# Gate and up weights of a mixture of experts in rows of 16 KB and transfers of 2 MB

## The chip, the cores and the metric

The kernel runs on one core of a Trainium2 chip. The core has a matrix engine (PE, TensorE), a vector engine (DVE), a scalar engine (ACT), GpSimd (POOL) and a sync engine (SP) that issues transfers; 16 DMA engines move data between HBM and the on-chip memory SBUF. The metric is the time of one execution on the device in microseconds (us), the median of several runs.

## The reference, cut to what matters

A trunk of two layers on 256 tokens of width 1024, all in float32. Each layer mixes the tokens in three parallel branches (one wide input projection, three token mixers, an output projection), adds a LayerNorm, and then runs a mixture of 32 experts, of which a token uses two:

```python
def _hier_moe(x, w_rg, b_rg, w_re, b_re, w_gate, w_up, w_down):
...
    for e in range(N_EXPERTS):
        h = jax.nn.silu(xt @ w_gate[e]) * (xt @ w_up[e])
        y = y + combine[:, e:e + 1] * (h @ w_down[e])
    return y.reshape(bsz, s, d)
```

`w_gate` and `w_up` are 1024 x 512 for each expert, `w_down` is 512 x 1024: 2 MB each, so 6 MB for an expert and 192 MB for a layer's experts. All of them are read in each execution.

## The kernel before

A layer has two stages. In the **mixer stage** PE multiplies the activations with the input projection and the branch projections, whose weights come in transfers of 512 KB (rows of 4 KB for each of 128 partitions): 76 of `w_in` and 24 of `w_br` in a layer. In the **expert stage** the 32 experts go in eight sets i = 0 to 7 of four experts (`EQ`). A set moves 8 MB of gate weights, 8 MB of up weights and 8 MB of down weights.

For a set, `set_front` builds a one-hot matrix `oh` that picks up to 32 tokens for each of the four experts, and its `gather` multiplies it with `x` (tile `pxg`, copied into `xg`), so that each expert's tokens stand in 32 columns. `set_mlp` multiplies `xg` with the gate weights (tile `pg`) and with the up weights (tile `pu`); the loop over the eight pieces k of the 1024 channels is outside, the loop over the four experts inside. `hr` is silu(gate) times up. `set_tail` transposes it (`pht`, `ht`) and multiplies it with the down weights in two halves (`pdn`, `os`), and `set_scatter` adds the result onto the tokens (`acc`). Set 4 begins behind a branch (`overflow`), for the case that an expert has more tokens than places; it isn't taken with these inputs. The last set's down weights come in smaller pieces (1/2 MB and 1/4 MB). After the last set come LayerNorm and the next layer's mixers.

A transfer of gate or up weights (`W`) takes 1 MB: `rows(src, u)` reads two pieces of an expert's weights as 128 rows of 8 KB. So a partition holds other channels than a plain tile would; `ROW(k)` gives the matching permutation of the channels of `x` for the gather, in pieces of 64 columns.

All weights go through a ring of places in SBUF (`ring`, list `places`): 24 places of 8 KB a partition, 9 of them always there (`wp`), and 6, 2 and 7 (`wb`, `wd`, `wc`) that are opened when the mixers' buffers are closed (`more_places`, at the positions `AT`) and closed again by `fewer_places` after the last set. A new transfer waits until the last reader of its place is done. SP issues all transfers in one order; a transfer that waits holds up those behind it. A transfer also waits for an earlier one through its completion counter, of which there are eight in turn (`DMAHW0` to `DMAHW7` in the order rows), so up to eight are in flight.

The order in which each engine's instructions stand is not written by hand: a scheduler of the framework sets it from the program when it is built. Two other loads matter below: `mixer_constants` reads `mc`, 128 rows of 9,500 bytes (1187.5 KB) that the next layer's mixers use, into the memory that the closed pools leave; `W_ln` reads the LayerNorm's parameters into a place of the ring.

Of the kernel before, what the change touches and what calls it, by code (L numbers as in the profile page):

```python
# [10 lines left out]
F32 = mybir.dt.float32  # L11
# [11 lines left out]
KD = D // 128  # L23
EPS = 1e-6
ALPHA = (2 * L) ** 0.25
NE = 32
WP, WB, WC = 9, 6, 7
SP, MX, MS, MB, WD = 8, 20, 6, 4, 2
AT = 4, 6, 7
AHEAD = 2  # L30
HP = 15
BUSY = 3
# [4 lines left out]
EQ = 4  # L37
# [79 lines left out]
def bc(ap, n):  # L117

    return ap.to_broadcast(list(ap.shape[:-1]) + [n])
# [42 lines left out]
def trunk_kernel(ctx: ExitStack, tc: tile.TileContext, x_in, w_in, w_br, w_g, w_u, w_d, smalls, lnp, consts, out,  # L162
                 dbg=None, layers=L, thresh=PL):
    nc = tc.nc
# [6 lines left out]
    wp = ctx.enter_context(tc.tile_pool(name="wp", bufs=WP))  # L171
# [3 lines left out]
    cnt = [0]  # L175
    pools = {}

    def open_pool(name, bufs, side):
        cnt[0] += 1
        cm = tc.tile_pool(name=f"{name}{cnt[0]}", bufs=bufs, side=side, reuse_waits="tile")  # L180
        pools[name] = (cm, cm.__enter__())

    def close_pool(name):
        pools.pop(name)[0].__exit__(None, None, None)
# [15 lines left out]


    places = ["wp"] * WP

    def ring(name="w"):
        cnt[0] += 1
        k = places.pop(0)
        places.append(k)
        return (wp if k == "wp" else pools[k][1]).tile([128, 2048], F32, name=f"{name}{cnt[0]}", tag="w")

    def more_places(name, n, side, at):  # L210
        open_pool(name, n, side)
        places[at:at] = [name] * n
# [2 lines left out]
        close_pool(name)  # L215
        places[:] = [k for k in places if k != name]

    def rows(src, u):

        return src[u:u + 2].rearrange("u p f -> (u p f)").rearrange("(q f) -> q f", f=2048)  # L220

    def ROW(k):

        u, j, kk = k // 4, k // 2 % 2, k % 2
        return lambda a: [a.rearrange("p (u h k q j) -> p u h k q j", h=2, k=2, q=64, j=2)[:, u, h, kk, :, j] for h in range(2)]

    def W(src):
        w = ring()
        nc.sync.dma_start(w, src)
        return w  # L230

# [28 lines left out]
    def mm(o, l, r, start=True, stop=True):  # L260
        return PE.matmul(o, l, r, start=start, stop=stop)  # L261

    def act(o, i, f=AF.Copy, **k):
        return ACT.activation(o, i, f, **k)  # L264
# [6 lines left out]
    def tap(name, ap):  # L271
        if dbg is not None and name in dbg:
            nc.sync.dma_start(dbg[name], ap)
# [7 lines left out]
    x = cp.tile([128, NT, D], F32, name="x")  # L281
# [121 lines left out]
    for l in range(layers):  # L403
# [676 lines left out]
        src = {n: w_in[l, i] for i, (n, _) in enumerate(BLOCKS)}  # L1080
# [94 lines left out]
        def after(n):  # L1175
# [27 lines left out]
            if n == "mC1":  # L1203
                close_pool("mb")
                open_pool("hq", 4, "right")
                more_places("wd", WD, "left", AT[1])
            if n == "o0":
                gb.append(W_ln(l, 0))
            if n == "mA":
                wv.drain("C")  # L1210
                close_pool("mc")
                close_pool("mx")
                more_places("wb", WB, "left", AT[0])

# [21 lines left out]
        close_pool("sb")  # L1236
        more_places("wc", WC, "left", AT[2])
        tap("x1", x)
# [74 lines left out]


        def set_front(i):
            e = EQ * i
            oh = T("oh")
            ohv = oh.rearrange("p (u t e s) -> p u t e s", u=2, t=2, e=EQ)
            it = C["iota"][:, None, None, 0:PL].to_broadcast([128, 2, EQ, PL])
            DVE.tensor_tensor(ohv[:, 0], it, bc(pv[:, :, e:e + EQ, None], PL), op=OP.is_equal)  # L1320
            POOL.tensor_mul(ohv[:, 1], ohv[:, 0], bc(cv[:, :, e:e + EQ, None], PL))  # L1321

            def gather(k0, n, copy, pin=False):

                p, t = P("pxg"), T("xg")
                for k in range(n):
                    for tt in range(NT):
                        for hh, xc in enumerate(ROW(k0 + k)(x[:, tt])):
                            m = mm(p[64 * hh:64 * hh + 64, k * 128:(k + 1) * 128], xc,
                                   oh[:, tt * 128:(tt + 1) * 128], tt == 0, tt == 1)  # L1330
                            if pin and k + tt + hh == 0:
                                tc.keep_in_program_order(m)
                copy(t[:, :n * 128], p[:, :n * 128])
                return [t[:, k * 128:(k + 1) * 128] for k in range(n)]

            def back():
                pt = P("pct")
                for tt in range(NT):
                    PE.transpose(pt[:, tt * 128:(tt + 1) * 128], oh[:, 256 + tt * 128:256 + (tt + 1) * 128], ident)
                ct = T("pct")  # L1340
                act(ct[:, :256], pt[:, :256])
                return ct

            return gather, back

        def set_mlp(i, xg, more=None):
            e = EQ * i
            pg, pu = P("pg"), P("pu")
            for p, src in ((pg, w_g), (pu, w_u)):
                for k in range(KD):  # L1350
                    if k == len(xg):
                        xg += more(k)
                    if k % 4 == 0:
                        ws = [W(rows(src[l, e + a], k // 2)).rearrange("p (k f) -> p k f", k=4) for a in range(EQ)]
                    for a in range(EQ):
                        ps = slice(PL * a, PL * a + PL)
                        mm(p[ps], xg[k][:, ps], ws[a][:, k % 4], k == 0, k == KD - 1)
            h = T("h")
            s = act(h, pg, AF.Silu)
            if i == NB - 1:  # L1360
                ln_exp_after(s)

            hr = T("hr")
            for hh in range(2):
                v = lambda a: a.rearrange("p (h k q j) -> p h k q j", h=2, k=2, q=64)[:, hh]
                DVE.tensor_mul(hr.rearrange("p (j k h q) -> p h k q j", j=2, k=2, h=2)[:, hh], v(h), v(pu))  # L1366
            return hr
# [41 lines left out]
        def overflow(mxi):  # L1409
            cov = M(64, "lg")  # L1410
            DVE.tensor_scalar(cov, posm, thresh + 0.5, None, op0=OP.is_gt)
            DVE.tensor_mul(cov, cov, cmb)
            covv = cov.rearrange("p (t e) -> p t e", t=2)
            rv = nc.values_load(mxi[0:1, 0:1], min_val=0, max_val=S)
            with tc.If(rv > thresh):
                with tc.For_i(0, NE, 1) as ei:

                    room = [wp.tile([128, 2048], F32, name=f"wo{cnt[0]}_{j}", tag="w") for j in range(WP)]
                    ws = []
                    for src in (w_g, w_u, w_d):  # L1420
                        ws.append([])
                        for u in range(4):
                            if u % 2 == 0:
                                both = room.pop()
                            w = both[:, u % 2 * 1024:u % 2 * 1024 + 1024]
                            POOL.dma_start(w, src[l, bass.ds(ei, 1), u].rearrange("e p f -> p (e f)"))
                            ws[-1].append(w)
                    for tt in range(NT):
                        own = [o[:, c:c + 512] for o in (room.pop(),) for c in (0, 512, 1024, 1536)]
                        xt = x_T(tt, own[:2])  # L1430
                        pg, pu = P("og"), P("ou")
                        for p, w in ((pg, ws[0]), (pu, ws[1])):
                            for k in range(KD):
                                mm(p, xt(k), w[k // 2][:, k % 2 * 512:k % 2 * 512 + 512], k == 0, k == 7)
                        h = own[2]
                        act(h, pg, AF.Silu)
                        DVE.tensor_mul(h, h, pu)
                        pt = P("opt")
                        for f in range(4):
                            PE.transpose(pt[:, f * 128:(f + 1) * 128], h[:, f * 128:(f + 1) * 128], ident)  # L1440
                        ht = own[3]
                        DVE.tensor_copy(ht, pt)
                        for hf in range(2):
                            po = P("opd")
                            for f in range(4):
                                mm(po, ht[:, f * 128:(f + 1) * 128],
                                   ws[2][2 * hf + f // 2][:, f % 2 * 512:f % 2 * 512 + 512], f == 0, f == 3)
                            DVE.tensor_scalar_mul(own[hf], po, covv[:, tt, bass.ds(ei, 1)])
                            mm(pacc[tt, hf], ident, own[hf], False, False)

        gather, back = set_front(0)
        xg = gather(0, 2, DVE.tensor_copy) + gather(2, 2, act)
# [12 lines left out]
        for i in range(NB):  # L1465
# [4 lines left out]
            if i == 0:  # L1470

                h = set_mlp(i, xg, lambda k: gather(k, k, act, True))
                ct = back()
                mxi = largest()
            else:
                ct, xg = nxt
                h = set_mlp(i, xg)
            if i + 1 < NB:
                gather, back = set_front(i + 1)
                xg = gather(0, 4, DVE.tensor_copy) + gather(4, 4, act)  # L1480
# [83 lines left out]
```

## Time and profile before

| | |
|---|---|
| median of 3 runs | 1631.17 us (1630.39 to 1631.46) |
| the profiled execution's own time | 1631.13 us |
| its span, first to last instruction | 1629.5 us |
| busy share of PE / DVE / ACT / POOL | 84% / 39% / 31% / 12% |
| mean rate of the DMA engines | 318 GB/s over the span |
| layer 0: mixers, experts | about 18 to 365 us, 385 to 812 us |
| layer 1: mixers, experts | about 823 to 1173 us, 1193 to 1630 us |

The profiled execution stands 0.04 us from the median, so sums made against its time hold for the median too. The span leaves out 1.6 us around the first and last instruction. The stages' limits are the times between which PE or the DMA engines work without a break; between them lie the LayerNorms, the router and the first one-hot matrices.

### The profile page before, as it was taken

What the parts mean: (1) busy time and instruction counts of PE and PEld (TensorE: products, weight loads), DVE (VectorE), ACT (ScalarE), POOL (GpSimd) and SP (SyncE); (2) the same over time, 40 slices, a digit from 0 to 9 for tenths busy, and PEclk for the clock granted to TensorE, in tenths of its full rate; (3) what the DMA queues carried; (4) which work ended last, traced back from release to release, by engine and by line L of the source; (5) the groups of instructions that cost most, each with busy time, mean ns of one, the idle gap of its engine ahead of it and who ended that gap; (6) DMA issues with size and microseconds to landing.
All of it is one profiled execution on the core that took longest, in us unless ns stands there. A gap on an engine that the chain in (4) does not pass through costs nothing.

```text
span 1629.5 us, 25989 instructions
## 1 busy us (share of the span) xinstructions
PE 1371.3 (84%) x10670; PEld 877.0 (54%) x10670; DVE 634.8 (39%) x1194; ACT 504.1 (31%) x997; POOL 188.2 (12%) x158
## 2 busy tenths in 40 slices
PE   8999999999877728866799999999998677287775
PEld 8999878985312203211289998799843122132211
DVE  6887777763000000000188887776620000000002
ACT  5846657541000000000067565685310000000000
POOL 0230243200000000000014212422000000000000
PEclk9999999999989959989899999999999999699889
DMA  9543333879999999999984443348799999999996
GB/s 382 182 155 130 129 131 105 317 292 411 427 427 426 427 426 426 426 427 426 409 318 132 144 141 104 134 141 346 293 408 427 428 425 426 427 427 426 427 427 257
DMA packets 90411, 518.96 MB, mean 318 GB/s; under 512 B 10032, under 2 KB 10672, under 8 KB 42928
## 3 DMA queue, kind: packets, MB, share of 16 engines
q1 hardware_dynamic: 90288, 517.25, 78.9%
q8 instruction: 86, 1.41, 0.3%
q14 instruction: 37, 0.30, 0.1%
HBM read 516.16 MB, written 1.05 MB: 317 GB/s over the span
## 4 chain that ended last, share of the span: by engine, by line
DMA 49%; PE 46%; DVE 3%; issue 1%; ACT 1%; SPq 0%; DVEq 0%
DMA w<-in_w_u_dram 19%; DMA w<-in_w_g_dram 14%; DMA w<-in_w_d_dram 14%; PE g L261 9%; PE pbr L261 6%; PE cx L261 3%; PE cz L261 3%; PE pout L261 3%; PE aq L261 1%; PE cbc L261 1%; PE av L261 1%; PE bq L261 1%; PE ak L261 1%; PE az L261 1%; PE bg L261 1%; PE pdn L261 1%
## 5 line engine op out<-in xcount | busy, mean ns | idle before, releaser
L252 DVE TENSOR_TENSOR hi<-w,hi 128x512 fp32r<-128x512 f32 x400 | 324.5, 828 | 84.2 <-ACT hi L264 37.4
L1366 DVE TENSOR_TENSOR hr<-h,pu 128x256 f32<-128x256 f32 x32 | 16.7, 599 | 726.7 <-PE pu L261 726.7
L264 ACT ACTIVATE hi<-w 128x512 fp32r<-128x512 f32 x400 | 242.8, 629 | 144.1 <-PE pbr L261 35.8
L261 PE MATMUL pg<-w,xg 128*32 128x512 f32 x1024 | 190.4, 667 | 114.4 <-DMA w<-in_w_g_dram 114.2
L261 PE MATMUL pu<-w,xg 128*32 128x512 f32 x1024 | 194.1, 673 | 61.1 <-DMA w<-in_w_u_dram 61.1
L261 PEld LDWEIGHTS pg<-w,xg 128*32 128x32 f32 x1024 | 43.7, 119 | 245.7 <-issue 138.2
L261 PE MATMUL pdn<-w,ht 128*32 128x512 f32 x1024 | 145.6, 614 | 26.5 <-DMA w<-in_w_d_dram 13.7
L261 PEld LDWEIGHTS pu<-w,xg 128*32 128x32 f32 x1024 | 45.6, 120 | 190.1 <-DMA w<-in_w_u_dram 110.0
L261 PE MATMUL g<-xh,hi 128*128 128x256 f32 x768 | 143.4, 285 | 0.0
L261 PEld LDWEIGHTS g<-xh,hi 128*128 128x128 f32 x768 | 120.7, 191 | 6.2 <-issue 5.8
L264 ACT ACTIVATE h<-pg 128x512 f32<-128x512 f32 x16 | 9.6, 597 | 338.7 <-PE pg L261 338.7
L261 PE MATMUL g<-xl,hi 128*128 128x256 f32 x384 | 108.9, 284 | 0.0
L261 PEld LDWEIGHTS pdn<-w,ht 128*32 128x32 f32 x1024 | 36.4, 112 | 121.8 <-issue 71.7
L1321 POOL TENSOR_TENSOR oh<-oh,cmb 128x256 f32<-128x256 f32 x16 | 10.0, 623 | 760.2 <-DVE oh L1320 654.9
L261 PE MATMUL pbr<-yh,hi 128*128 128x256 f32 x512 | 95.4, 283 | 0.0
L264 ACT ACTIVATE xg<-pxg 128x512 f32<-128x512 f32 (+1 forms) x18 | 10.3, 574 | 247.5 <-PE pxg L261 247.5
L264 ACT ACTIVATE os<-pdn 128x512 f32<-128x512 f32 x32 | 19.1, 596 | 215.7 <-PE pdn L261 140.9
L261 PEld LDWEIGHTS pbr<-yh,hi 128*128 128x128 f32 x512 | 80.4, 190 | 0.8 <-issue 0.3
L261 PE MATMUL pxg<-oh,x 128*64 128x128 f32 x1024 | 59.9, 274 | 21.9 <-DVE oh L1320 18.3
L261 PEld LDWEIGHTS pxg<-oh,x 128*64 128x64 f32 x1024 | 56.0, 138 | 34.9 <-issue 26.2
L261 PEld LDWEIGHTS g<-xl,hi 128*128 128x128 f32 x384 | 73.5, 191 | 0.1
L261 PE MATMUL pbr<-yl,hi 128*128 128x256 f32 x256 | 73.0, 285 | 0.0
(351 smaller groups left out, 2209.2 us busy)
## 6 DMA issues: line engine op xcount, KB each, us to landing
w<-in_w_g_dram SPq DMA_DIRECT2D x128, 1024.0 KB, 19.5
w<-in_w_u_dram SPq DMA_DIRECT2D x128, 1024.0 KB, 19.6
w<-in_w_d_dram SPq DMA_DIRECT2D x112, 1024.0 KB, 19.6
w<-in_w_in_dram SPq DMA_DIRECT2D x152, 512.0 KB, 4.7
w<-in_w_br_dram SPq DMA_DIRECT2D x48, 512.0 KB, 4.7
w<-in_w_d_dram SPq DMA_DIRECT2D x24, 512.0 KB, 11.8
ln<-in_lnp_dram SPq DMA_DIRECT2D x8, 512.0 KB, 10.7
w<-in_w_d_dram SPq DMA_DIRECT2D x16, 256.0 KB, 7.5
```

The lines of the kernel that those rows point to most:

```text
L252: return DVE.tensor_sub(l, src, lo(h))
L261: return PE.matmul(o, l, r, start=start, stop=stop)
L264: return ACT.activation(o, i, f, **k)
L1321: POOL.tensor_mul(ohv[:, 1], ohv[:, 0], bc(cv[:, :, e:e + EQ, None], PL))
L1366: DVE.tensor_mul(hr.rearrange("p (j k h q) -> p h k q j", j=2, k=2, h=2)[:, hh], v(h), v(pu))
```

## The change

Twelve places of 16 KB take the place of 24 places of 8 KB; the memory is the same. `unit` hands out a whole place, `ring` half of one, two in a row from the same place. Sets 1 to 7 load gate and up weights with `W2`: one transfer of 2 MB for an expert's whole matrix, 128 rows of 16 KB. Set 0 keeps its transfers of 1 MB. The gather of sets 1 to 7 works in pieces of 32 columns instead of 64, twice as many. Down weights, mixer weights and LayerNorm parameters keep their transfers, in halves of a place; a place is free again only when both halves are read.

```diff
-WP, WB, WC = 9, 6, 7
-SP, MX, MS, MB, WD = 8, 20, 6, 4, 2
-AT = 4, 6, 7
+WP, WB, WC = 4, 3, 4
+SP, MX, MS, MB, WD = 8, 24, 6, 4, 1
+AT = 2, 3, 4
...
-    def ring(name="w"):
+    halves = []
+
+    def unit(name="w"):
+
+        assert not halves
         cnt[0] += 1
         k = places.pop(0)
         places.append(k)
-        return (wp if k == "wp" else pools[k][1]).tile([128, 2048], F32, name=f"{name}{cnt[0]}", tag="w")
+        return (wp if k == "wp" else pools[k][1]).tile([128, 4096], F32, name=f"{name}{cnt[0]}", tag="w")
+
+    def ring(name="w"):
+
+        if not halves:
+            w = unit(name)
+            halves.extend((w[:, 0:2048], w[:, 2048:4096]))
+        return halves.pop(0)
...
-    def rows(src, u):
-
-        return src[u:u + 2].rearrange("u p f -> (u p f)").rearrange("(q f) -> q f", f=2048)
-
-    def ROW(k):
-
-        u, j, kk = k // 4, k // 2 % 2, k % 2
-        return lambda a: [a.rearrange("p (u h k q j) -> p u h k q j", h=2, k=2, q=64, j=2)[:, u, h, kk, :, j] for h in range(2)]
+    def rows(src, u, n=2):
+
+        return src[u:u + n].rearrange("u p f -> (u p f)").rearrange("(q f) -> q f", f=1024 * n)
+
+    def ROW(k, n):
+
+        u, j, kk = k // (2 * n), k // 2 % n, k % 2
+        return lambda a: [a.rearrange("p (u h k q j) -> p u h k q j", h=n, k=2, q=128 // n, j=n)[:, u, h, kk, :, j]
+                          for h in range(n)]
...
+    def W2(src):
+        w = unit()
+        nc.sync.dma_start(w, src)
+        return w
...
-            e = EQ * i
+            e, nr = EQ * i, 2 if i == 0 else 4
...
-                    if k % 4 == 0:
+
+                    if i == 0 and k % 4 == 0:
                         ws = [W(rows(src[l, e + a], k // 2)).rearrange("p (k f) -> p k f", k=4) for a in range(EQ)]
+                    elif k == 0:
+                        ws = [W2(rows(src[l, e + a], 0, 4)).rearrange("p (k f) -> p k f", k=8) for a in range(EQ)]
                     for a in range(EQ):
                         ps = slice(PL * a, PL * a + PL)
-                        mm(p[ps], xg[k][:, ps], ws[a][:, k % 4], k == 0, k == KD - 1)
+                        mm(p[ps], xg[k][:, ps], ws[a][:, k % (4 if i == 0 else 8)], k == 0, k == KD - 1)
```

The diff leaves out three lines of the gather that use `nr` and one that cuts the places of the branch into halves. The order of the instructions changes at some places; three follow. In the rows `w_…` are places of the ring, `in_w_g_dram`, `in_w_u_dram` and `in_w_d_dram` the gate, up and down weights in HBM; the shape is that of the transfer or of the operand.

**SP at the end of layer 0.** The last down weights of set 7, then the next layer's loads (`sb` and `mc` are the mixers' small parameters and constants). Before:

```order
L1377 DMA w_6579<-in_w_d_dram 128x512
L538 DMA w_6711<-in_w_in_dram 128x1024 x2
L538 DMA w_6782<-in_w_in_dram 128x1024 x2
L538 DMA w_6889<-in_w_in_dram 128x1024 x2
L294 DMA sb_6628<-in_smalls_dram 128x393
L538 DMA w_6997<-in_w_in_dram 128x1024 x2
L538 DMA w_7076<-in_w_in_dram 128x1024 x2
L538 DMA w_7155<-in_w_in_dram 128x1024 x2
L538 DMA w_7234<-in_w_in_dram 128x1024 x2
L538 DMA w_7335<-in_w_in_dram 128x1024 x2
L538 DMA w_7462<-in_w_in_dram 128x1024 x2
L300 DMA mc_6887<-in_consts_dram 128x2375
```

Of the change, the same place:

```order
L1396 DMA w_6618<-in_w_d_dram 128x1024 x2
L1396 DMA w_6618<-in_w_d_dram 128x512 x4
L316 DMA mc_6926<-in_consts_dram 128x2375
L1396 DMA w_6619<-in_w_d_dram 128x1024 x2
L1396 DMA w_6619<-in_w_d_dram 128x512 x4
L554 DMA w_6751<-in_w_in_dram 128x1024 x4
L310 DMA sb_6668<-in_smalls_dram 128x393
```

`mc` stood behind the last down weights and 18 transfers of `w_in`; it now stands ahead of the last 2 MB of down weights.

**PE and SP in layer 0's set 7.** SP's transfers of the change for set 7, gate (`g`) and up (`u`) weights and the LayerNorm's parameters (`ln`):

```order
L245 DMA w_6497<-in_w_g_dram 128x4096
L245 DMA w_6531<-in_w_u_dram 128x4096
L245 DMA w_6533<-in_w_u_dram 128x4096
L245 DMA w_6535<-in_w_u_dram 128x4096
L253 DMA ln_6486<-in_lnp_dram 128x1024 x2
L245 DMA w_6491<-in_w_g_dram 128x4096
L245 DMA w_6493<-in_w_g_dram 128x4096
L245 DMA w_6495<-in_w_g_dram 128x4096
L245 DMA w_6537<-in_w_u_dram 128x4096
L1396 DMA w_6589<-in_w_d_dram 128x1024 x4
```

PE's first matmuls of that set, in the change:

```order
L277 MATMUL pg_6489<-w_6491,xg_6351 32x512
L277 MATMUL pu_6490<-w_6531,xg_6351 32x512
L277 MATMUL pu_6490<-w_6533,xg_6351 32x512
L277 MATMUL pu_6490<-w_6535,xg_6351 32x512
L277 MATMUL pg_6489<-w_6493,xg_6351 32x512
L277 MATMUL pg_6489<-w_6495,xg_6351 32x512
L277 MATMUL pg_6489<-w_6497,xg_6351 32x512
L277 MATMUL pg_6489<-w_6491,xg_6351 32x512
```

Before, SP loaded the set's eight transfers of gate, then eight of up weights, and PE could do half of `pg` with the first four. Now PE's sixth matmul needs the gate place `w_6495`, the seventh of the set's eight gate and up transfers, and 29 matmuls of `pg` and 29 of `pu` stand behind it.

**SP and PE in set 4, around the branch.** Behind the branch SP of the change issues:

```order
L245 DMA w_5810<-in_w_g_dram 128x4096
L245 DMA w_5814<-in_w_g_dram 128x4096
L245 DMA w_5816<-in_w_g_dram 128x4096
L240 DMA w_6013<-in_w_d_dram 128x2048 x2
L245 DMA w_6076<-in_w_u_dram 128x4096
```

Set 4's other gate place `w_5812`, its four up places and six of its eight transfers of down weights stand ahead of the branch. PE's first matmuls of the set, in the change:

```order
L277 MATMUL pg_5808<-w_5810,xg_5523 32x512
L277 MATMUL pg_5808<-w_5812,xg_5523 32x512
L277 MATMUL pu_5809<-w_5850,xg_5523 32x512
L277 MATMUL pu_5809<-w_5852,xg_5523 32x512
```

Set 4 was split by the branch before, too: three gate, seven up and five down transfers of 1 MB ahead of it, the other five gate, one up and three down behind it. In the change PE's first matmul of the set needs a place that is loaded behind the branch, and the whole of the set's work stands behind that matmul; `w_6076` is set 5's first.

## Rows read from the trace of the kernel before

**Rows 1.** The page: span, busy shares, tracks of PE and DMA, the chain's shares.

```profile
span 1629.5 us, 25989 instructions
PE 1371.3 (84%) x10670; PEld 877.0 (54%) x10670; DVE 634.8 (39%) x1194; ACT 504.1 (31%) x997; POOL 188.2 (12%) x158
...
PE   8999999999877728866799999999998677287775
...
DMA  9543333879999999999984443348799999999996
...
DMA 49%; PE 46%; DVE 3%; issue 1%; ACT 1%; SPq 0%; DVEq 0%
```

**Rows 2.** Windows of the four stages: busy us, PE's clock, DMA share, GB/s.

```profile
18.00:365.00 347.00, 345.35 (x2986) 314.39 (x2986) 268.08 (x478) 216.58 (x432) 85.14 (x66) 1.00 0.54 195
385.00:812.00 427.00, 311.44 (x2104) 104.41 (x2105) 23.59 (x46) 24.49 (x43) 4.32 (x7) 0.90 1.01 424
823.00:1173.00 350.00, 349.39 (x3033) 318.33 (x3022) 271.82 (x485) 218.47 (x435) 86.33 (x67) 1.00 0.51 185
1193.00:1630.00 437.00, 307.39 (x2100) 101.70 (x2096) 29.96 (x58) 25.16 (x45) 7.40 (x9) 0.91 0.97 409
```

**Rows 3.** The chain that ended last, in layer 0's experts: start, us, what.

```profile
428.13 19.54 DMA w<-in_w_d_dram
...
447.73 19.56 DMA w<-in_w_g_dram
...
467.35 19.56 DMA w<-in_w_u_dram
```

**Rows 4.** What SP waited for, 400 to 760 us: us, times, longest.

```profile
SPq L229 <- DMA w<-in_w_u_dram: 99.2, 48, 2.5
SPq L229 <- DMA w<-in_w_g_dram: 96.4, 47, 3.2
SPq L229 <- DMA w<-in_w_d_dram: 95.0, 46, 2.2
SPq L229 <- PE pu L261: 6.2, 5, 4.8
```

**Rows 5.** Windows with rows of 4 KB (the first) and of 8 KB (the others).

```profile
826.00:832.00 6.00, 6.00 (x53) 6.00 (x52) 4.80 (x14) 3.92 (x11) 0.00 (x0) 1.00 1.02 422
440.00:560.00 120.00, 90.52 (x552) 27.32 (x547) 5.35 (x10) 5.33 (x10) 1.23 (x2) 0.90 1.01 426
611.20:616.00 4.80, 4.80 (x50) 2.20 (x47) 0.00 (x0) 0.00 (x0) 0.00 (x0) 1.00 1.03 434
606.00:611.20 5.20, 5.11 (x25) 1.73 (x28) 0.00 (x0) 0.00 (x0) 0.00 (x0) 0.50 1.00 424
580.50:611.20 30.70, 5.11 (x25) 1.73 (x28) 0.00 (x0) 0.00 (x0) 0.00 (x0) 0.50 1.01 427
```

**Rows 6.** The chain at the end of layer 1: last set and LayerNorm.

```profile
1551.22 2.56 PE pdn L261 x21
1553.78 20.26 DMA w<-in_w_g_dram
...
1574.10 19.51 DMA w<-in_w_u_dram
...
1593.62 9.97 DMA w<-in_w_d_dram
...
1603.66 8.18 DMA w<-in_w_d_dram
...
1611.88 3.68 PE pdn L261 x28
```

**Rows 7.** DMA packets, 829.9 to 830.6 us, while `mc` lands among `w_in`.

```profile
DMA packets 51, 0.29 MB, mean 408 GB/s; under 512 B 5, under 2 KB 5, under 8 KB 33
```

**Rows 8.** Tile `mc`: forms, counts, ns min/median/max, first and last start.

```profile
L300 SPq DMA_DIRECT2D mc<-in_consts_dram x2: 327/484/642, 6.2 to 821.0; - x2
L261 PE MATMUL cum<-ev,mc x16: 197/282/283, 45.5 to 853.6; 128*128 128x40 f32 x16
```

**Rows 9.** Timeline of PE in layer 1's last set: idle time before in brackets.

```profile
1593.65 3.62 PE L261 MATMUL pu<-w,xg 128*32 128x512 f32 x26 [1.46 <-DMA w<-in_w_u_dram]
...
1599.97 3.41 PE L261 MATMUL pdn<-w,ht 128*32 128x512 f32 x22 [0.78 <-DVE ht L1385]
...
1611.88 3.63 PE L261 MATMUL pdn<-w,ht 128*32 128x512 f32 x28 [2.24 <-DMA w<-in_w_d_dram]
```

**Rows 10.** Timeline of PE behind the branch of set 4, layer 0.

```profile
606.09 1.07 PE L261 MATMUL pg<-w,xg 128*32 128x512 f32 x3 [28.32 <-DMA w<-in_w_g_dram]
```

**Rows 11.** DMA issues on the page: KB each, median us from issue to landing.

```profile
w<-in_w_in_dram SPq DMA_DIRECT2D x152, 512.0 KB, 4.7
```

**Rows 12.** Groups of the page: the gather's matmuls.

```profile
L261 PE MATMUL pxg<-oh,x 128*64 128x128 f32 x1024 | 59.9, 274 | 21.9 <-DVE oh L1320 18.3
```

More of the change, by code (lines that the diff above doesn't have):

```diff
@@ L1327, in gather @@
                     for tt in range(NT):
-                        for hh, xc in enumerate(ROW(k0 + k)(x[:, tt])):
-                            m = mm(p[64 * hh:64 * hh + 64, k * 128:(k + 1) * 128], xc,
+                        for hh, xc in enumerate(ROW(k0 + k, nr)(x[:, tt])):
+                            m = mm(p[128 // nr * hh:128 // nr * (hh + 1), k * 128:(k + 1) * 128], xc,
                                    oh[:, tt * 128:(tt + 1) * 128], tt == 0, tt == 1)
@@ L1416, in overflow @@
                 with tc.For_i(0, NE, 1) as ei:
-                    room = [wp.tile([128, 2048], F32, name=f"wo{cnt[0]}_{j}", tag="w") for j in range(WP)]
+                    room = [wp.tile([128, 4096], F32, name=f"wo{cnt[0]}_{j}", tag="w") for j in range(WP)]
+                    room = [r[:, c:c + 2048] for r in room for c in (0, 2048)]
                     ws = []
```

## The prediction

> **What bounds the kernel now.** The page comes first: PE is busy for 84% of the span, yet the tracks show two alternating regimes, PE full while the DMA engines are at about a half, then the DMA engines full while PE is at 7 to 8 tenths; the chain that ended last is 49% DMA and 46% PE [rows 1]. The windows of the four stages say it sharply: in the mixers PE works 345.35 of 347 us and 349.39 of 350 us with a DMA share of 0.54 and 0.51; in the experts the DMA share is 1.01 and 0.97 and PE is busy for 311.44 of 427 us [rows 2]. So a better transfer is worth nothing in the mixers and its full length in the experts. There the chain is a row of transfers, each eight deep: 8 MB about every 19.6 us (428.13, 447.73, 467.35), which is 2.4525 us for 1 MB or 427 GB/s [rows 3]. SP waits there for earlier transfers, 48, 47 and 46 times, and for PE's reads of a place only five times, 4.8 us at most [rows 4]: places are not short.
>
> **The change, part by part.**
>
> *Longer rows.* 2 x 7 x 8 = 112 transfers of 2 MB replace 224 of 1 MB: 224 MB of the 384 MB that the experts take. No transfer of before has rows of 16 KB, so the price comes from the step from 4 to 8 KB, by two roads. By the chain: eight transfers of 1/2 MB with rows of 4 KB took 9.97 us, eight of 1 MB with rows of 8 KB 19.51 to 19.56 [rows 3, 6], 2.49 and 2.445 us for 1 MB. That step saves 0.05 us per MB for half the rows; if the excess is a cost per row or per transfer, halving again saves half of it, 0.025 x 224 = 5.7 us. By the rates: 422 GB/s in a window of rows of 4 KB and 427 in windows of rows of 8 KB (426 in the longest) [rows 5] are 2.485 and 2.456 us per MB; half of 0.029 by 224 is 3.3 us. I take **-4.4**, the middle. The bounds: 0, if a row beyond 8 KB is cut or gains nothing; and the highest rate of a short window, 434 GB/s [rows 5], which makes 2 MB last 4.832 instead of 4.905 us, 112 x 0.073 = 8.2 us. I see no loss here: while `mc`'s rows of 9,500 bytes land among rows of 4 KB, 18 of 51 packets are of 8 KB or more, at 408 GB/s in so short a window [rows 7], so longer rows go through whole.
>
> The row at hand: 1 MB takes 2.45 us in the stream, and 1 MB at 427 GB/s takes 2.456, so a single transfer's own start-up doesn't show with eight in flight [rows 3, 5]. The Trainium skill gives a fixed cost of about 2.0 us for each transfer beside its bytes ("DMA: Bandwidth & Descriptors", section "Anatomy of one DMA — SWDGE (gpsimd) path", for transfers issued by GpSimd). Were that laid end to end, 112 transfers fewer would save an estimated 224 us by that page of the skill; the trace disagrees for this stream, and the sum goes by the rows.
>
> *`mc` moves.* Its 1187.5 KB stood behind the last down weights and 18 mixer transfers, where the DMA engines are half idle; now they stand ahead of layer 0's last 2 MB of down weights, on which the end of the layer hangs. At 427 GB/s that is **+2.85 us** of the DMA-bound stage. It buys nothing: `mc` was issued at 821.0 and is first read by PE at about 853 us in layer 1 (in layer 0, 6.2 and 45.5) [rows 8], and PE hardly idles in either mixer stage [rows 2]. It waits for a place that `pg` of the last set frees, some 10 us ahead of its turn, so no further wait is priced. Layer 1 has no such load.
>
> *The last set.* With T the end of set 6's last transfer (1551.22 in layer 1), PE ended its last matmuls at 1611.88 + 3.68 = T + 64.3, a little behind the last piece of weights [rows 6]. In the change PE's sixth matmul needs 15 MB after T (four gate places, three up places and 1 MB of parameters, by the order), T + 36.8 us; 118 records (59 matmuls of two) then follow at one go. The nearest burst after a long pause is that of set 4: after 28.32 us of idleness the first 5.2 us had a granted clock of 0.50 (1.2 GHz) and 25 records, the next 4.8 us 1.00 (2.4 GHz) and 50 [rows 5, 10]. So 25 records in 5.2 us and 93 in 8.9, to T + 50.9; 2.7 us for `hr`, `pht` and `ht` (1597.27 to 1599.97 [rows 9]); `pdn` starts at about T + 54 instead of T + 48.75. Its first half (32 records, 4.4), the scatter (2.0) and the second half (4.1) end at T + 64.5; the transfers alone would end it near T + 64.0. **+0.5** in layer 1 (0 to 3); in layer 0 `mc` delays the weights by more than that, so 0.
>
> *Set 4.* PE's first matmul waits for a transfer behind the branch, 18 MB after set 3's last, +44.1 us. Of the matmuls behind it the up weights' 32 free the places of set 5's first transfers: about 67 records, 5.2 us at half clock and 4.0 at full, +53.5. The stream runs dry at 24 MB, +58.9; a transfer of 1/2 MB that found a short queue landed 4.7 us after its issue, 1.2 of it bytes [rows 11], so a place is needed by about +55.4. Slack 2 us: **0** (bound: all at half clock, +58, a hole of 2.6 us in each layer).
>
> *The gather.* 64 records more in seven sets of each layer, at 274 ns and overlapped: 59.9 us busy for 1024 [rows 12], so up to 3.7 us more of PE in a set. In the expert stages PE idles for over 115 us of 427 [rows 2], 14 us in a set; that hides it. The steady sets also wait longer for whole 2 MB places and then run in bursts, but places were not short before [rows 4], and twelve larger ones hold the same 24 MB. In the mixers places come free in larger lots; a dozen blocks stand loaded ahead of PE by the order, and one lands 4.7 us after its issue [rows 11]: 0.
>
> **Sum:** 1631.13 - 4.4 + 2.85 + 0.5 = **1630.1 us**, also against the median, which lies 0.04 away.
>
> **The rivals.** (1) *Long rows run at the best rate seen.* For it: 434 GB/s in one window of 4.8 us [rows 5]; against: the window of 120 us has 426. It gives 1631.13 - 8.2 + 3.35 = 1626.3 us. The Trainium skill puts the fabric's ceiling at 435.2 GB/s ("DMA: Bandwidth & Descriptors", section "Where 436 GB/s comes from"); the trace lies below it by 2%, so there is room, but not much more than this rival uses. (2) *Rows of 16 KB gain nothing,* because what is left of the excess hangs on bytes or on HBM: 427 GB/s already is close to the best window [rows 5]; `mc` and the burst remain, 1631.13 + 3.35 = 1634.5 us. (3) *Half clock for longer, slower.* PE's waits grow, one place being 4.9 us of transfer instead of 2.45, and its bursts at the end of the last set and in set 4 lie on the path. 5.2 us more at half clock (25 records, 2.4 us at full) cost 2.8. It decides at about 13 us of half clock in the last burst instead of 5.2, then the loss passes +3.3; with a hole of 2 us in one set 4 some +5, **1635 us**; with every record of both last sets at half clock PE ends at T + 81, and the time near 1660. For it: the windows of the experts have a mean clock of 0.90 and 0.91; against: the burst of set 4 recovered within 5.2 us [rows 2, 5]. By the Trainium skill short work between long waits for transfers brings TensorE back to half rate every time ("TensorE: Matmul & The Clock Gate", section "HAM oscillation — how this bites in real kernels"); the trace agrees for the long pause (0.50), and no run here shows it for 59 matmuls at one go.
>
> **How the numbers follow.** Forecast (around 1630) 0.52, rival 1 0.2, rival 2 0.15, rival 3 0.13. 0.2% (3.3 us) is about what a measurement of this kernel tells from no change: the borders are 1627.9 and 1634.4. The forecast's own range is 1628.5 to 1632.5 (rate -5.7 to -3.3, burst 0 to 3, set 4). Faster: rival 1 and a little of the forecast, 0.23. Slower: rival 3 and most of rival 2, 0.23. Same: 0.54. The range for 8 in 10 reaches from 1625.3, rival 1 without a burst's cost and a little more, to 1636.5, the usual size of rival 3.
>
> **What would show it.** In the new trace 16 MB of gate and up weights should take about 38.6 to 38.9 us instead of 39.2; `mc` should be issued before the last down weights of layer 0 and the layer's end move by the balance; the mixers should keep their 347 and 350 us; PE's window behind the third gate place of a last set should show half clock for about 5 us. Wrong it would be if the long rows moved by another rate, if SP waited for PE in the experts (a hole in the DMA share near set 4 or 5), or if the mixers' places, now in pairs, came late and PE waited for `w_in`.

## The result, and the profile after

The changed kernel takes 1642.12 us (median of 4 runs), the kernel before 1630.78 us in the same comparison: the ratio is 1.007 with a 95% interval of 1.0058 to 1.0082. It is slower by 11.3 us, above the range (1625.3 to 1636.5), where the prediction gave slower 0.23 and about the same 0.54. Its profiled execution took 1641.85 us; the span is 1640.2 us, 10.7 us longer than before.

The page of the changed kernel: span, track of the DMA engines, shares of the chain.

```profile
span 1640.2 us, 27442 instructions
...
DMA  9443324869999999999963442348699999999995
...
PE 49%; DMA 47%; DVE 2%; ACT 1%; issue 1%; SPq 0%; DVEq 0%
```

The stages are as before [rows 1], but where a mixer stage ends and an expert stage begins (slices 9 and 29 of the track) the digit is 6 instead of 7. The windows of the four stages, with the columns of [rows 2] and at the same times (layer 1 comes some 5 us later now, so its two windows cover slightly other work):

```profile
18.00:365.00 347.00, 345.09 (x2984) 313.89 (x2982) 269.07 (x477) 216.68 (x429) 85.12 (x66) 1.00 0.50 188
385.00:812.00 427.00, 280.61 (x2518) 102.69 (x2514) 22.14 (x42) 23.38 (x41) 4.60 (x8) 0.84 1.01 427
823.00:1173.00 350.00, 348.47 (x3068) 316.78 (x3068) 270.95 (x480) 221.21 (x439) 86.18 (x66) 1.00 0.47 174
1193.00:1630.00 437.00, 286.57 (x2600) 106.30 (x2595) 24.25 (x48) 24.36 (x43) 4.32 (x7) 0.84 0.99 418
```

PE's work in the mixers is untouched, and layer 0's experts move their bytes at a higher rate, 427 instead of 424 GB/s. But the mixer stages now move less, 188 and 174 GB/s instead of 195 and 185: bytes of the next stage that were loaded there are loaded later. In layer 0 that is 2.3 MB less over 347 us. More than half of it is seen in the last 11 us of layer 0's mixers. The window of 352.5 to 361.3 us of the changed kernel:

```profile
352.50:361.30 8.80, 8.80 (x40) 7.26 (x39) 4.94 (x11) 0.41 (x2) 0.00 (x0) 1.00 0.14 33
```

The same window of the kernel before:

```profile
352.50:361.30 8.80, 8.80 (x40) 7.18 (x40) 4.94 (x10) 0.00 (x0) 0.00 (x0) 1.00 0.54 199
```

PE works through it in both. The DMA engines are nearly idle after the change (0.14) where they had half a load before (0.54); at the end of layer 1's mixers it is the same (0.15, 1166.7 to 1175.5 us, against 0.53 before). The window holds 1.4 MB less; most of the rest is missing before 300 us (159 GB/s from 18 to 300 us, before 165). The timeline of SP says which transfers are missing; of the changed kernel (start, us from the first to the last of the row's issues, transfers):

```profile
333.46 12.03 SPq L240 DMA_DIRECT2D w<-in_w_d_dram  x4
359.07 5.90 SPq L240 DMA_DIRECT2D w<-in_w_u_dram  x8
366.59 4.86 SPq L240 DMA_DIRECT2D w<-in_w_d_dram  x4
```

and of the kernel before:

```profile
334.99 19.19 SPq L229 DMA_DIRECT2D w<-in_w_d_dram  x5
360.60 0.33 SPq L229 DMA_DIRECT2D w<-in_w_g_dram  x1
363.51 2.98 SPq L229 DMA_DIRECT2D w<-in_w_u_dram  x6
368.12 2.29 SPq L229 DMA_DIRECT2D w<-in_w_d_dram  x2
```

All are transfers of 1 MB of set 0. After the change 12 of its 24 MB are issued at 359 us or later, before it was 9. SP stands there for places in the memory of the mixers' own buffers, which PE's `pout` matmuls read to the end (three waits between 340 and 375 us, 13.0 us together, against 9.2). Eight of the 12 MB go into the four places of `wc` (7 MB before, in seven places), and four into the two places in which a LayerNorm vector of 4 KB a partition holds half a place of 16 KB (2 MB before, in two places of 8 KB). PE reached set 0 no later: its first gate matmuls begin 16.4 us behind the mixers' last matmul in both kernels (379.75 and 381.30 us); the stream of set 1 was late. The chain of the changed kernel, the mixers' last matmuls and the pieces that end with the first 8 MB of set 1, in both layers:

```profile
341.38 21.97 PE pout L277 x96
...
389.31 22.69 DMA w<-in_w_u_dram
...
1155.58 21.97 PE pout L277 x96
...
1203.51 22.46 DMA w<-in_w_u_dram
```

and of the kernel before:

```profile
342.92 21.97 PE pout L261 x96
...
392.49 15.94 DMA w<-in_w_u_dram
...
1150.78 21.97 PE pout L261 x96
...
1199.67 16.50 DMA w<-in_w_u_dram
```

That is 412.00 against 408.43 us and 1225.97 against 1216.17 us. Counted from the mixers' last matmul, the first 8 MB of set 1 are there after 48.65 and 48.42 us instead of 43.54 and 43.42: **5.1 us late in layer 0 and 5.0 in layer 1**. At 2.45 us for 1 MB the 3 MB that wait besides would be 7.4 us; it is less because the kernel before did not load at the full rate there either (387 GB/s from 361.3 to 392 us, now 428).

With PE's last down matmuls of layer 0, in the changed kernel

```profile
807.69 4.28 PE L277 MATMUL pdn<-w,ht 128*32 128x512 f32 x28
```

and before

```profile
805.51 2.34 PE L261 MATMUL pdn<-w,ht 128*32 128x512 f32 x16
```

and the first `ps` matmuls of layer 1 on the two chains (827.33 against 822.49 us) the whole difference of the two profiled executions can be laid out:

| from ... to | before, us | after, us | difference |
|---|---|---|---|
| start to set 1's first 8 MB, layer 0 | 408.43 | 412.00 | +3.57 |
| to PE's last down matmul, layer 0 | 399.42 | 399.97 | +0.55 |
| to layer 1's `ps` matmuls | 14.64 | 15.36 | +0.72 |
| to set 1's first 8 MB, layer 1 | 393.68 | 398.64 | +4.96 |
| to PE's last down matmul, layer 1 | 399.39 | 400.31 | +0.92 |
| sum | 1615.56 | 1626.28 | +10.72 |

So +8.5 of the 10.7 us lie where set 0 is loaded. The first row would be +5.1 had the mixers of layer 0 not ended 1.5 us earlier in this execution (363.35 against 364.89 us); how much of that belongs to the change isn't shown, since over the builds shown below this time lies between 361.9 and 364.3 us. Rows two and five are balances. In layer 1 the last weights landed 395.7 us behind set 1's first 8 MB instead of 397.8, so the longer rows took some 2.1 us, and PE ended 4.6 us behind them instead of 1.6: its burst in the last set added some 3. For layer 0 the split is only worked out: a gain of some 2.3 us by the longer rows and 2.85 us for `mc` make the +0.55. Of `mc`, which stands ahead of the last down weights now:

```profile
L316 SPq DMA_DIRECT2D mc<-in_consts_dram x2: 328/472/616, 5.7 to 796.7; - x2
```

It was issued at 821.0 us before [rows 8]. And PE's timeline at the end of layer 1, after the landing of the third gate place:

```profile
1597.14 9.14 PE L277 MATMUL pg<-w,xg 128*32 128x512 f32 x58 [3.01 <-DMA w<-in_w_g_dram]
...
1606.15 7.43 PE L277 MATMUL pu<-w,xg 128*32 128x512 f32 x56
...
1616.27 4.49 PE L277 MATMUL pdn<-w,ht 128*32 128x512 f32 x36 [0.79 <-DVE ht L1404]
...
1622.60 3.63 PE L277 MATMUL pdn<-w,ht 128*32 128x512 f32 x28
```

No bracket stands behind the last row: PE no longer waits for the last down weights, as it did for 2.24 us before [rows 9]. Its own work is what ends last. Two windows of that burst:

```profile
1597.10:1606.30 9.20, 9.16 (x64) 2.38 (x66) 0.00 (x0) 0.00 (x0) 0.00 (x0) 0.72 1.00 415
1606.30:1613.60 7.30, 7.28 (x60) 1.92 (x52) 0.00 (x0) 1.88 (x2) 0.00 (x0) 1.00 1.03 416
```

### The profile page after: what moved, and what is told of

The parts are those of the page before. It is cut to its first block, busy times and chain, and to the rows that moved or that the text cites. A ratio compares the mean times of both kernels' runs of the same rounds, so it can differ in the third digit from the quotient of the medians.

```text
span 1640.2 us, 27442 instructions
## 1 busy us (share of the span) xinstructions
PE 1319.1 (80%) x11566; PEld 880.4 (54%) x11566; DVE 634.7 (39%) x1194; ACT 504.5 (31%) x997; POOL 188.2 (11%) x158
## 4 chain that ended last, share of the span: by engine, by line
PE 49%; DMA 47%; DVE 2%; ACT 1%; issue 1%; SPq 0%; DVEq 0%
DMA w<-in_w_d_dram 21%; DMA w<-in_w_g_dram 14%; DMA w<-in_w_u_dram 11%; PE g L277 9%; PE pbr L277 6%; PE cx L277 3%; PE cz L277 3%; PE pout L277 3%; PE pg L277 2%; PE pu L277 2%; PE cbc L277 1%; PE aq L277 1%; PE av L277 1%; PE bq L277 1%; PE ak L277 1%; PE az L277 1%
## 5 line engine op out<-in xcount | busy, mean ns | idle before, releaser
L268 DVE TENSOR_TENSOR hi<-w,hi 128x512 fp32r<-128x512 f32 x392 | 319.2, 830 | 83.4 <-ACT hi L280 36.0
L277 PE MATMUL pg<-w,xg 128*32 128x512 f32 x1024 | 178.9, 690 | 212.8 <-DMA w<-in_w_g_dram 212.8
L280 ACT ACTIVATE hi<-w 128x512 fp32r<-128x512 f32 x392 | 238.2, 628 | 141.0 <-PE pbr L277 42.8
L277 PE MATMUL pu<-w,xg 128*32 128x512 f32 x1024 | 167.0, 685 | 32.4 <-DMA w<-in_w_u_dram 32.3
L277 PE MATMUL pdn<-w,ht 128*32 128x512 f32 x1024 | 127.3, 601 | 14.7 <-DVE ht L1404 12.7
L277 PE MATMUL pxg<-oh,x 128*32 128x128 f32 (+1 forms) x1920 | 61.8, 279 | 25.2 <-DVE oh L1336 21.7
L277 PEld LDWEIGHTS pxg<-oh,x 128*32 128x32 f32 (+1 forms) x1920 | 57.8, 139 | 37.8 <-issue 28.1
L277 PE MATMUL acc<-os,pct 128*128 128x512 f32 x128 | 62.7, 625 | 9.6 <-ACT os L280 5.2
```

What stands on the lines that cost most here:

```text
L268: return DVE.tensor_sub(l, src, lo(h))
```

## The experiments

The theory after the first reading (A): the larger places cost the time, because set 0 then waits for the mixers' last reads with 12 MB instead of 9 MB. The rival (B): the 2 MB transfers cost it, because places come free later. A second question was what makes the rate, the length of a row or the size of a transfer. Each ratio is to runs of the kernel before taken beside it, whose median lay between 1630.46 and 1631.68 us; differences between experiments carry about 1 us of that.

**1. Small transfers in large places.** Set 1 to 7 as set 0 is.

```diff
-            e, nr = EQ * i, 2 if i == 0 else 4
+            e, nr = EQ * i, 2
...
-                    if i == 0 and k % 4 == 0:
+                    if k % 4 == 0:
...
-                    elif k == 0:
-                        ws = [W2(rows(src[l, e + a], 0, 4)).rearrange("p (k f) -> p k f", k=8) for a in range(EQ)]
...
```

> The changed kernel with its twelve places of 16 KB, but gate and up weights of all sets again in transfers of 1 MB with rows of 8 KB (two to a place) and the gather in pieces of 64 columns. Theory A (places): the larger places alone delay set 0, because 12 MB instead of 9 MB of it wait for the mixers' last reads, so set 1's stream starts some 5 us late in each layer as in the changed kernel, 16 MB go at the old 39.2 us, and the last set has no burst: about 1644 us (1642.1 + 5.0 - 3.1). Theory B (transfers): the 2 MB transfers make places come free late at the start of set 1; without them only the moved constants remain, about 1634 us.

Measured: 1644.78 us, ratio to before 1.0088 (1.0071 to 1.0105). With transfers, rows and gather as before the loss is there, and larger, as theory A said (about 1644): the 2 MB transfers are not its cause. The idle stretch is too, its window from this run:

```profile
352.50:361.30 8.80, 8.80 (x40) 7.25 (x39) 4.97 (x10) 0.41 (x2) 0.00 (x0) 1.00 0.08 14
```

**2. Transfers of 2 MB with rows of 8 KB.** One transfer for an expert's matrix, two rows for each partition; the gather in pieces of 64 columns.

```diff
-        nc.sync.dma_start(w, src)
+        nc.sync.dma_start(w.rearrange("p (t f) -> p t f", t=2),
+                          src.rearrange("(t u) p f -> t (u p f)", t=2).rearrange("t (q f) -> q t f", f=2048))
...
-            e, nr = EQ * i, 2 if i == 0 else 4
+            e, nr = EQ * i, 2
...
```

> The changed kernel with transfers of 2 MB whose rows in HBM are 8 KB again (two rows for a partition) and the gather in pieces of 64 columns. If the length of a row sets the rate, 2 MB take 4.905 us instead of 4.86 and the time is about 1647 us; if the size of a transfer sets it, 4.86 us and 1642 us.

Measured: 1645.73 us, ratio 1.0091 (1.0074 to 1.0108): 3.6 us above the changed kernel, where 5 was expected if the row counts and 0 if the transfer does. A window of 120 us in set 1 to 3 says the same, of this run

```profile
440.00:560.00 120.00, 83.15 (x540) 25.64 (x540) 5.33 (x11) 5.33 (x10) 1.23 (x2) 0.83 1.01 427
```

and of the changed kernel

```profile
440.00:560.00 120.00, 82.37 (x668) 25.87 (x668) 4.80 (x9) 5.33 (x10) 1.23 (x2) 0.83 1.01 429
```

With rows of 8 KB experiment 1 has 427 GB/s there as well, the kernel before 426 [rows 5]; with rows of 16 KB experiments 4, 6, 9, 11 and 12 have 429 too. The length of the row makes the rate; doubling the size of a transfer alone does nothing that can be seen.

**3. Rows of 16 KB in transfers of 1 MB,** that is of 64 partitions each.

```diff
-        nc.sync.dma_start(w, src)
+        for q in (0, 64):
+            nc.sync.dma_start(w[q:q + 64], src[q:q + 64])
```

> The changed kernel with rows of 16 KB, each 2 MB cut into two transfers of 64 partitions, 1 MB each. If the length of a row sets the rate, 2 MB take 4.86 us and the time stays at 1642 us; if the size of a transfer sets it, 4.905 us and 1647 us.

Measured: 2222.09 us, ratio 1.3645 (1.3582 to 1.3708). Neither held: it took a third longer. A window among its gate and up transfers:

```profile
600.00:625.00 25.00, 8.05 (x16) 1.29 (x11) 0.00 (x0) 0.60 (x1) 0.00 (x0) 0.70 1.01 222
```

The DMA engines are busy (1.01) at 222 GB/s: transfers into half the partitions, the two halves in turn, move at half the rate. As a test of row against transfer it was useless. The Trainium skill states the halving beforehand ("SBUF — State Buffer", section "Door 1: The DMA port swizzle (why `[64,N]` ≈ `[32,N]`)"): 64 partitions in a row reach eight of the memory's 16 ports. The run agrees, with 222 against 429 GB/s. Why the two halves don't add up, though transfers into both are under way, no run here shows.

**4. The LayerNorm's vectors in one half place.**

```diff
-        assert not halves
+        halves.clear()
...
-        r = []
+        r, w = [], ring("ln")
         for j in range(2):
-            r.append(ring("ln")[:, 0:1024])
+            r.append(w[:, 1024 * j:1024 * j + 1024])
```

> The changed kernel with the two LayerNorm vectors in one half place instead of in two halves of two places, so that one place fewer is held until the LayerNorm has read them. Theory A (places): 10 to 11 MB instead of 12 MB of set 0 wait for the mixers' end, set 1's stream starts 2.5 to 5 us earlier in each layer, about 1636 us (1632 to 1637). Theory B (transfers): no change, 1642 us.

Measured: 1638.53 us, ratio 1.0049 (1.0032 to 1.0065): 3.6 us less than the changed kernel, less than the 6 expected (1632 to 1637 us), but not the nothing of theory B. SP's timeline of this run at the point in question:

```profile
359.91 5.38 SPq L240 DMA_DIRECT2D w<-in_w_u_dram  x7
365.33 4.86 SPq L240 DMA_DIRECT2D w<-in_w_d_dram  x3
...
384.25 0.33 SPq L240 DMA_DIRECT2D w<-in_w_d_dram  x1
```

It is 11 MB instead of 12, one of them behind PE's first gate matmuls: 1 MB, 2.45 us at most in a layer. That fits 3.6 us for two layers.

**5. The constants late.** `mc` is issued after the last down weights' transfer (in the build four transfers of `w_in` stand between).

```diff
...
-        nc.sync.dma_start(mc, consts[:, C_STAY:])
+        with (tc.issue_after(R0.pop("down").ins) if "down" in R0 else contextlib.nullcontext()):
+            nc.sync.dma_start(mc, consts[:, C_STAY:])
...
-                    nc.sync.dma_start(w[:, c:d], r[:, c:d])
+                    R0["down"] = nc.sync.dma_start(w[:, c:d], r[:, c:d])
```

> The changed kernel with the mixers' constants issued behind the last down weights of layer 0 and four transfers of w_in. If the constants alone delay layer 0's end, as the prediction priced them, the time falls by 2.85 us to about 1639.3 us. If PE's burst of the last set, which ended its own work near 811.3 us against 812.0 us measured, takes their place, it falls by 0.7 us only, to 1641.4 us.

Measured: 1639.22 us, ratio 1.006 (1.0043 to 1.0076): 2.9 us less than the changed kernel, the prediction's price. The trace shows that it isn't quite that. Layer 0's last down matmuls of this run,

```profile
807.75 3.63 PE L278 MATMUL pdn<-w,ht 128*32 128x512 f32 x28
```

begin as late as in the changed kernel (807.69) and end 0.6 us earlier: the last set's burst holds them, with `mc` or without; the scatter and the layer's boundary gain more, so that the last `ps` matmuls stand 1.84 us earlier (825.73 against 827.57). The rest of the 2.7 us in the span comes in the last set of layer 1, which the edit doesn't touch.

**6. The last set in small transfers.** Set 7 as set 0: 1 MB, rows of 8 KB.

```diff
-            e, nr = EQ * i, 2 if i == 0 else 4
+            e, nr = EQ * i, 2 if i in (0, NB - 1) else 4
...
```

with the same condition in the loads.

> The changed kernel with set 7 loaded as set 0 is: transfers of 1 MB, rows of 8 KB, gather in pieces of 64 columns. If the burst behind the third gate place holds the end of layer 1 (PE ended 4.3 us behind the last landing, before 1.2), the time falls by 3.1 us less 0.6 for the shorter rows, to about 1639.6 us; in layer 0 the constants cover it. If the end hangs on something else, 1642.7 us.

Measured: 1640.1 us, ratio 1.0061 (1.0045 to 1.0078), 2.0 less than the changed kernel where 2.5 was expected. PE waits for the down weights again and ends at 1623.75 instead of 1626.23 us:

```profile
1620.13 3.62 PE L277 MATMUL pdn<-w,ht 128*32 128x512 f32 x26 [0.20 <-DMA w<-in_w_d_dram]
```

**7. The kernel before, its vectors in one place of 8 KB.** The edit of experiment 4.

> The kernel before with the two LayerNorm vectors in the two halves of one place of 8 KB instead of in two places. Theory A (what waits for the mixers' end sets the start of set 1): 8 MB instead of 9 MB of set 0 wait, 2.45 us earlier in each layer, about 1625.6 us. Theory B (only larger places or transfers cost): no change, 1630.5 us.

Measured: 1631.89 us, ratio 1.0008 (0.9998 to 1.0017): no gain, against theory A as it was put. The window of this run at the start of set 1 shows why:

```profile
381.90:384.30 2.40, 2.40 (x44) 1.93 (x44) 0.00 (x0) 0.38 (x1) 0.00 (x0) 1.00 0.54 140
```

Set 0 has landed, SP issues set 1's first transfers at 381.98 us, when PE's first gate matmuls of set 0 free a place, and the DMA engines have nothing for a while (0.54). Set 1 starts at the later of two: the end of set 0's waiting part, and PE's first reads of set 0. The kernel before had them nearly at one time, so taking from the first gains nothing there; the change moved it by 5 us.

**8. Experiments 4, 5 and 6 together.**

> The changed kernel with the LayerNorm vectors in one half place, the constants behind the last down weights, and set 7 in transfers of 1 MB. If the three costs are separate: 3.6 us as measured with the vectors alone, 2.85 us for the constants now that no burst takes their place, 2.5 us for the burst in layer 1, so about 1633 us. The rest above the kernel before would be the 2 MB of set 0 that still wait more than before, less the gain of the rows of 16 KB.

Measured: 1632.27 us, ratio 1.0009 (1.0000 to 1.0019): 9.9 us less than the changed kernel, where the three alone gave 3.6, 2.9 and 2.0. They add up, about as expected (1633).

**9. The vectors in 8 KB of their own,** in a small pool that is closed before `wc` is opened.

```diff
         r = []
+        if i == 0:
+            open_pool("ln", 1, "left")
+            w = pools["ln"][1].tile([128, 2048], F32, name=f"ln{l}", tag="ln")
         for j in range(2):
-            r.append(ring("ln")[:, 0:1024])
+            r.append(ring("ln")[:, 0:1024] if i else w[:, 1024 * j:1024 * j + 1024])
...
+        close_pool("ln")
...
```

> The changed kernel with the first LayerNorm's vectors in 8 KB of their own outside the ring, so that 8 MB of set 0 wait for the mixers' last reads instead of 12 MB. If set 1's stream starts when the waiting part has landed, but not before PE's first reads of set 0 free places (which is what capped the kernel before with one place for the vectors), it starts near 387.3 us instead of 392.6 us in layer 0 and as much earlier in layer 1: about 1631.5 us. If the 12 MB aren't the cause, 1642 us.

Measured: 1640.02 us, ratio 1.0053 (1.0039 to 1.0066), where 1631.5 was expected. 8 MB waited as planned, but for longer. The window of this run:

```profile
361.30:369.50 8.20, 7.95 (x46) 6.04 (x44) 7.52 (x18) 1.49 (x4) 0.00 (x0) 1.00 0.00 0
```

The first of the four new places takes over the vectors' memory and so waits until the LayerNorm has read them (SP issues at 369.7 us), and the three others stand behind it on SP: no transfer at all for 8 us. (The scheduler also put `mc` behind the last down weights in this build, at 807.0 us.)

**10. Experiment 9 with 5 and 6.**

> As the run before, with the constants behind the last down weights and set 7 in transfers of 1 MB too. 1632.3 us were measured with those two and the vectors in one half place; set 1's stream started 3.5 us late there against the kernel before, in each layer. Without that: about 1625 us, 5 to 6 us under the kernel before, by the gain of the rows of 16 KB in six sets.

Measured: 1635.53 us, ratio 1.0025 (1.0015 to 1.0036), where 1625 was expected. It shares the flaw of experiment 9.

**11. As 9, but the place over the vectors' memory is used last.**

```diff
-        more_places("wc", WC, "left", AT[2])
+        more_places("wc0", 1, "left", AT[2])
+        more_places("wc", WC - 1, "left", AT[2])
...
```

> As the run with the vectors in 8 KB of their own, but the one place of the ring that later takes over this memory is used last of the four that come free at the mixers' end. There the first of the four waited until 369.7 us for the LayerNorm's reads and held up the other three on SP. Now 6 MB can start at about 360 us and 2 MB at 370 us, with 16 MB of set 0 already loaded, so set 1's stream should start at about 387 us (PE's first reads of set 0 set it) instead of 392.6 us, and as much earlier in layer 1: about 1631 us. If what waits for the mixers' end isn't the cause: 1640 to 1642 us.

Measured: 1632.06 us, ratio 1.0005 (0.9996 to 1.0014): 10 us less than the changed kernel, with all its transfers of 2 MB. The windows of this run:

```profile
352.50:361.30 8.80, 8.80 (x40) 7.24 (x39) 4.87 (x12) 0.41 (x2) 0.00 (x0) 1.00 0.59 233
361.30:369.50 8.20, 7.78 (x50) 5.81 (x48) 6.52 (x14) 2.09 (x5) 0.00 (x0) 1.00 0.70 272
```

The hole is filled again (0.59 against 0.14). `mc` was late in this build too (801.5 us), so some of the 10 us are its. The cleanest comparison is with experiment 9, which has `mc` late as well and whose program differs in the order of the four places alone: 8.0 us. Against experiment 5, with `mc` late and set 0 as in the change, it is 7.2.

**12. As 11, with 5 and 6.**

> As the run before, with the constants behind the last down weights and set 7 in transfers of 1 MB. 1632.3 us were measured with these two while set 1's stream started 3.5 us late in each layer against the kernel before; without that lateness about 1625 us, some 5 us under the kernel before. If larger places cost something else as well, no better than 1632 us.

Measured: 1627.62 us, ratio 0.998 (0.9971 to 0.9989): 3.6 us under the kernel before, the fastest of all, between the two expectations (1625 and 1632). 96 transfers of 2 MB remain in it; at 0.032 to 0.038 us each (experiment 2's 3.6 us for 112, or 2.1 us for a layer's 56) they would explain 3.1 to 3.6. Against the changed kernel less the 2.9 and 2.0 us of experiments 5 and 6 it is 9.6 us faster, near the 10.1 us that the traces give for the late stream of the two layers.

## Why the prediction was wrong, step by step

**The step that failed** is the last sentence on the gather: "In the mixers places come free in larger lots; a dozen blocks stand loaded ahead of PE by the order ...: 0". It asked whether the mixers' own weights would come late, which they didn't (PE is busy for 345.09 of 347 us), and not what else goes through the ring in that stage: all of set 0. Of it 3 MB more than before wait for the last reads of the mixers, while the DMA engines idle. The term put at 0 is 5.1 and 5.0 us counted from the mixers' end (+3.57 and +4.96, 8.5 of the 10.7 us, in the table). Experiment 1 shows the loss with the places alone, experiments 9 and 11 show 8.0 us for when the last four places come free and nothing else, and experiment 11 is within the uncertainty of the kernel before (with `mc` late). It had no rival either: the "hole" of rival 3 was looked for behind set 4, and the sign that the mixers' places, "now in pairs, came late" was tied to PE waiting for `w_in`, which it didn't.

**Longer rows:** right. -4.4 was forecast; the trace gives some 2.1 us in layer 1, and experiment 2 against the changed kernel 3.6 us for both layers. The prediction left open whether the excess hangs on rows or on transfers; experiment 2 shows that it is the rows. Rivals 1 and 2 fall: 429 GB/s over 120 us is neither 434 nor the 426 and 427 of rows of 8 KB.

**`mc`:** the price was right, the place only in part. Alone its removal gave 2.9 us in the median, but by the traces 1.84 at the layer's boundary and 0.6 at PE's last down matmul, because PE's burst ends there at nearly the same time. The prediction put the burst of layer 0 at nothing beside `mc`; the two are about equal.

**The last set:** the mechanism was right, the size wrong. +0.5 was forecast, about 3 stand in the balance, and its removal gave 2.0 in the median and 2.5 in the trace. The half clock (1.2 GHz) lasted as long as forecast: 0.72 over 9.2 us is 5.2 us at half. Mis-sized was the time at the full clock: 118 records took 16.4 us and not 14.1, since those at full clock went at about 0.12 us each (60 in 7.28 us). The 0.096 of the prediction was 50 records in one window of 4.8 us [rows 5]; why they went faster there no run shows.

**Set 4:** right. SP waited there for PE's reads for 20.7 us, and the DMA share stayed at 1.01 over 624 to 634 us: no hole. **The gather:** right; PE is busy for 280.61 of 427 us. **Rival 3:** the mean clock in the experts fell to 0.84 from 0.90 and 0.91, but the half clock of the last burst lasted no longer than forecast, and set 4 had no hole.

## What to carry to other kernels

A place of a ring is free when the last byte in it has been read, so doubling the size of the places doubles what one small or late reader holds: count, at each point where a buffer changes its owner, how many bytes must wait for it before and after, not only whether the total is the same. Where the bound changes from compute to transfers, the bytes loaded ahead of the border are worth up to their full transfer time (here 5 us in a layer for 3 MB, of 7.4), and the stretch to look at is the idle time of the DMA engines just ahead of it. And when the late part is cut, name what is late next: taking 1 MB from the kernel before gained nothing, because PE's first reads were due at the same time.

## What the runs showed of the hardware that was not expected

Transfers into 64 partitions, the two halves in turn, moved at 222 GB/s with all DMA engines busy (1.01), those into 128 partitions with the same rows of 16 KB at 429 GB/s. Rows of 16 KB are worth little over rows of 8 KB, 429 against 427 GB/s, and one transfer of 2 MB with two rows of 8 KB for a partition goes at the rate of two transfers of 1 MB.
